# Where the weights of a feature-major product lie: 320 and 64 bytes from x modulo 512, in place of 448 for both parts

## The chip, the cores and the metric

The kernel runs on one core of a Trainium2 chip. The metric is the device time of one execution in microseconds, as the median of several runs. On-chip memory (SBUF) has 128 partitions; all addresses here are byte addresses within a partition. Engines: PE is TensorE (PEld its weight loads), DVE is VectorE, ACT is ScalarE, POOL is GpSimd, SP issues most DMAs.

## The reference

A decoder trunk of two pre-norm residual layers over 256 tokens and 2048 features, all in float32:

```
for l in range(2):
    h = rmsnorm(x, norm_mix[l])
    x = x + (even_mixer if l == 0 else odd_mixer)(h, ...)
    h = rmsnorm(x, norm_ffn[l])
    x = x + conv_ffn(h, ffn_w_up[l], ffn_conv_w[l], ffn_w_down[l])
return rmsnorm(x, norm_final)

def conv_ffn(h, w_up, conv_w, w_down):
    g, u = split(h @ w_up)              # 2048 -> 2 x 5632
    g = causal_dwconv(g, conv_w)        # width 3
    return (silu(g) * u) @ w_down       # 5632 -> 2048
```

The even mixer is a dilated-window attention of 8 heads beside a convolution module of 1024 channels; the odd mixer is an attention of 16 heads with forget gates. Each has an input projection and an output projection. Nearly all the work is products of a [256 x K] activation with a [K x N] weight matrix that is read once from memory, some 410 MB in all.

## The kernel before, in words

Each float32 product is made from two parts of each operand: hi is the operand rounded to the format that TensorE reads in one pass (float32r), lo is the rest. A product is hi·hi + hi·lo + lo·hi, three matmuls.

`stream` brings the weights. For each 1 MB piece of a panel of 512 columns it issues a DMA into a `raw` tile (three buffers), then twice takes a half of it: ACT copies it to `whi` (line 103), DVE subtracts to get `wlo` (line 104). Each of `whi` and `wlo` has four buffers of 4608 bytes per partition, 4096 of them used; `split_pair` cuts the used part out, from element `shift` on. Such a pair feeds 24 matmuls of a feature-major product, a piece 48.

There are two forms of product:

- Feature-major, `panel_b`: the weights (128 x 128) are the stationary operand and x (128 x 256 tokens) is streamed; the result has features on the partitions. For each of four column blocks and each k tile there is whi with the hi part of x (line 117), whi with the lo part of x (line 118), wlo with the hi part of x (line 119). A panel over all 16 k tiles is 192 matmuls. All projections but v, and the up products of both layers and the down product of layer 0, are made so. It takes its weights with `shift=SHIFT`, 16 elements.
- Token-major, `panel_a` and the last down product of layer 1: a 128 x 128 block of x is stationary and 512 columns of weights are streamed (lines 123 to 125). It takes its weights with shift 0. The last few matmuls, of acc_e, use weights in other rooms as well: the buffers of `gp`, `cv`, `hp` and `raw`, which the FFN has no more use for.

The x of a product is `xs` (the normed residual stream), `y` (the mixers' outputs) or `hp` (the FFN's hidden values), with hi and lo 1024 bytes apart. Small pads (`PADS`) put all three at the same place: each starts 64 bytes past a multiple of 512. So do the `whi` and `wlo` tiles, and since 4608 is nine times 512, all of their buffers. Steps inside them are multiples of 512 as well (a block of 128 float32 is 512 bytes). So the distance between x and weights modulo 512, x minus weights, is one number for all feature-major matmuls: 64 - (64 + 64) = 448 with a shift of 16 elements. For the token-major ones the streamed weights less the stationary x are 0, and in the rooms at the end also 480 and 448 (`whi` in `gp`, two buffers).

Order: the Tile scheduler sets the order of each engine's instructions when the program is built. TensorE runs the panels one after another; the next weights are copied and subtracted ahead of need. Between the matmuls of a panel stand a few small ones of norms and attention (for instance the four of `ss_f` and two of `bc_f` in the first panel of each FFN).

Of the kernel before, what the change touches and what calls it, by code (L numbers as in the profile page):

```python
# [29 lines left out]
KC = 2  # L30
NEG = -1.0e30
PADS = {"y0": 288, "mx1": 192, "ff0": 128, "ff1": 64}
SHIFT = 16
UP_GROUPS = ((0, 6), (6, 11))
TWO_PI_PARTS = (6.28125, 0.0019340515136718750, 1.2554228305816650e-06, 6.0796790328e-10)
MAGIC = 12582912.0
# [7 lines left out]
def trunk(ctx, tc, a):  # L44
# [14 lines left out]
    def misc(name):  # L59
        return pms.tile([P, 512], F32, tag="misc", name=name)  # L60
# [16 lines left out]
    def fill_in(after):  # L77
        pace[1] += pace[0]
        with tc.issue_after(after.ins), tc.high_priority(offset=-BEHIND):
            while waiting and pace[1] >= 1:  # L80
                waiting.pop(0)()
                pace[1] -= 1
        pace[1] = min(pace[1], 1.0)

    def split_pair(nm, half, width, shift):
        both = [wp.tile([P, KC * 512 + 128], F32R, tag=w, name=f"{w}_{nm}") for w in ("whi", "wlo")]
        return [t[:, shift:shift + KC * 512].rearrange("p (k c) -> p k c", k=half) for t in both]

    def stream(src_of, nk, width, name, dk=4, room=None, shift=0):

        half = KC * 512 // width
        for c in range(0, nk, dk * 512 // width):
            n = dk * 512 // width
            raw = wp.tile([P, 2 * KC * 512], F32, tag="raw", name=f"raw_{name}_{c}", bufs=3)
            rv = raw[:, :n * width].rearrange("p (k c) -> p k c", k=n)
            loads.append(nc.sync.dma_start(out=rv, in_=src_of(c, n)))
            for h in range(0, n, half):
                if room is None:
                    hi, lo = split_pair(f"{name}_{c + h}", half, width, shift)
                else:  # L100
                    hi, lo = room(f"{name}_{c + h}")
                with tc.high_priority(offset=AHEAD):
                    S.copy(hi, rv[:, h:h + half, :])  # L103
                    last = V.tensor_tensor(out=lo, in0=rv[:, h:h + half, :], in1=hi.bitcast(F32), op=ALU.subtract)  # L104
                fill_in(last)
                yield list(range(c + h, c + h + half)), hi, lo

    def panel_b(src_of, x2, kts, name, order=(0, 1, 2, 3), dk=4):

        acc = {m: pacc.tile([P, 512], F32, tag="acc", name=f"acc_{name}_{m}") for m in order}  # L110
        for ks, hi, lo in stream(src_of, len(kts), P * len(order), name, dk, shift=SHIFT):
            for m in order:
# [9 lines left out]
    def mm_a(o, hi, lo, xh, xl, first, last):  # L122
        PE.matmul(o, xh, hi, start=first, stop=False)  # L123
        PE.matmul(o, xh, lo, start=False, stop=False)  # L124
        PE.matmul(o, xl, hi, start=False, stop=last)  # L125

    def panel_a(src_of, x2, kts, name):

        acc = [pacc.tile([P, 512], F32, tag="acc", name=f"acc_{name}_{t}") for t in range(2)]
        for ks, hi, lo in stream(src_of, len(kts), 512, name):  # L130
            for t in range(2):
                ts = slice(t * P, (t + 1) * P)
                for j, k in enumerate(ks):
                    x = x2(kts[k])
                    mm_a(acc[t], hi[:, j, :], lo[:, j, :], x[:, 0, ts], x[:, 1, ts], k == 0, k == len(kts) - 1)
        return acc

    def cols(w, panel, k0=0):

        def part(c, n):  # L140
            kt = k0 // P + c
            return w[panel, kt // 4, :, kt % 4:kt % 4 + n, :]
        return part
# [123 lines left out]
    with ExitStack() as ph:  # L267
# [72 lines left out]
        with tc.high_priority(offset=400):  # L340
            for i in range(4):
                t, h = divmod(i, 2)
# [259 lines left out]
    def x_back():  # L602
        for kt in range(0, KT, 2):
            tx = misc(f"tb_{kt}")
            for t in range(2):
                for k in range(2):
                    PE.transpose(tx[:, t * T + k * P:t * T + (k + 1) * P], xT[:, kt + k, t * P:(t + 1) * P], ident)
            S.copy(o[:, :, kt * P:(kt + 2) * P], tx.rearrange("p (t c) -> p t c", t=2))
        S.dma_start(out=gb, in_=a["norm_final"].partition_broadcast(P))

    def add_o(acc, t, i):
        cs = slice(512 * i, 512 * (i + 1))
        V.tensor_tensor(out=o[:, t, cs], in0=acc, in1=o[:, t, cs], op=ALU.add)

    def down1(gi, w_dn, k0, kts, g2, fp):
        if gi == 0:
            x_back()
            for i in range(4):
                acc = panel_a(cols(w_dn, i, k0=k0), g2, kts, f"d1{gi}{i}")
                for t in range(2):  # L620
                    add_o(acc[t], t, i)
            return


        with tc.issue_after(copies[-1].ins):
            S.activation(dummy, ones[:, 0:1], AF.Sqrt)
        acc = [[None, None] for i in range(4)]
        for b, (i, t) in enumerate((i, t) for i in range(4) for t in range(2)):
            acc[i][t] = misc(f"acc_e{i}{t}") if b < 3 else pacc.tile([P, 512], F32, tag="acc", name=f"acc_e{i}{t}")
        n = len(kts)  # L630

        def rows(i, t, at, ks, hi, lo):
            for j, k in enumerate(ks):
                kt, ts = kts[at + k], slice(t * P, (t + 1) * P)
                mm_a(acc[i][t], hi[:, j, :], lo[:, j, :], g2(kt)[:, 0, ts], g2(kt)[:, 1, ts], at + k == 0, at + k == n - 1)

        def part(i, at, k, **kw):
            return stream(cols(w_dn, i, k0=k0 + at * P), k, 512, f"e{i}_{at}", dk=k, **kw)

        for at in range(0, n - 4, 4):  # L640
            for i in range(4):
                for got in part(i, at, 4):
                    for t in range(2):
                        rows(i, t, at, *got)


        def from_gate(nm):
            return [fp.tile([P, KC, 512], F32R, tag=tag, name=f"{w}_{nm}", bufs=2) for tag, w in (("gp", "whi"), ("cv", "wlo"))]

        def from_hidden(nm):  # L650
            both = fp.tile([P, 4, 2, T], F32R, tag="hp", name=f"wboth_{nm}", bufs=6).rearrange("p a b t -> p (a b t)")
            return [both[:, 1024 * h:1024 * (h + 1)].rearrange("p (k c) -> p k c", k=KC) for h in range(2)]

        def from_weights(nm):
            return split_pair(nm, KC, 512, 0)

        def from_raw(nm):
            both = wp.tile([P, 2 * KC * 512], F32, tag="raw", name=f"wboth_{nm}", bufs=3).bitcast(F32R)
            return [both[:, 1024 * h:1024 * (h + 1)].rearrange("p (k c) -> p k c", k=KC) for h in range(2)]

        rooms = [from_gate] * 2 + [from_hidden] + [from_weights] * 4 + [from_raw]
        at = n - 4
        last = [list(part(i, at, 4, room=lambda nm: rooms.pop(0)(nm))) for i in range(4)]
        for t in range(2):
            for i in range(4):
                for got in last[i]:
                    rows(i, t, at, *got)
                add_o(acc[i][t], t, i)
                cs = slice(512 * i, 512 * (i + 1))
                S.activation(junk[:, 512 * (i % 2):512 * (i % 2) + 512], o[:, t, cs], AF.Square, accum_out=fs[:, t, i:i + 1])  # L670
                if i < 3:
                    V.tensor_tensor(out=o[:, t, cs], in0=o[:, t, cs], in1=gb[:, cs], op=ALU.mult)
            V.reduce_sum(out=sf[:, t:t + 1], in_=fs[:, t, :], axis=AX.X)
            rf = rsqrt_cols(sf[:, t:t + 1], 1.0 / D, f"fin{t}", 1)
            for i in (1, 0, 3, 2):
                cs = slice(512 * i, 512 * (i + 1))
                if i == 3:
                    V.scalar_tensor_tensor(out=o[:, t, cs], in0=o[:, t, cs], scalar=rf, in1=gb[:, cs], op0=ALU.mult, op1=ALU.mult)
                elif i == 1:
                    V.tensor_scalar(out=o[:, t, cs], in0=o[:, t, cs], scalar1=rf, scalar2=None, op0=ALU.mult)  # L680
                else:
                    S.activation(o[:, t, cs], o[:, t, cs], AF.Copy, scale=rf)
                nc.sync.dma_start(out=a["out"][t * P:(t + 1) * P, cs], in_=o[:, t, cs])
# [63 lines left out]
```

## Time and profile before

| | |
|---|---|
| median of 3 runs | 2223.23 us (2222.28 to 2224.14) |
| the profiled execution | 2224.01 us, of which the trace spans 2222.2 |
| PE busy | 2202.4 us, 99%, 17,210 matmuls |
| PEld busy | 2132.0 us, 96% |
| DVE, ACT busy | 1407.7 us (63%), 1052.3 us (47%) |
| DMA | 414.61 MB, 187 GB/s in the mean |
| granted TensorE clock | 0.998 in the mean |

A matmul's duration in the profile is longer than the time from its start to the next one's, since matmuls are pipelined: a busy PE is not PE at its peak. The pace of a stretch is its length divided by the matmuls in it. A group's row gives the line, engine, operation, tiles and shapes, how often, then total and mean duration.

### The profile page before, as it was taken

The numbers are of one execution on the slowest core, as the hardware profiler recorded it, in microseconds if no ns is written. First come the engines' busy times: TensorE is split into PE (matmuls) and PEld (weight loads), VectorE is DVE, ScalarE is ACT, GpSimd is POOL, SyncE is SP. The second block draws the span as 40 slices with busy tenths as digits, with TensorE's granted clock in tenths as the row PEclk, the third lists the DMA queues.
The fourth block names the chain that finished last, engine by engine and source line by source line (L and its number), as shares of the span: only waits on it lengthen the run. The fifth ranks groups of instructions, "written<-read, shape, count | busy, mean of one in ns | idle before, by whom it ended". The sixth has DMA issues, their size and how long they took to land.

```text
span 2222.2 us, 40343 instructions
## 1 busy us (share of the span) xinstructions
PE 2202.4 (99%) x17210; PEld 2132.0 (96%) x17210; DVE 1407.7 (63%) x2105; ACT 1052.3 (47%) x1370; POOL 15.5 (1%) x50
## 2 busy tenths in 40 slices
PE   8999999999999999999999999999999999999998
PEld 8999999999999999999999999999999988999986
DVE  6999986666644566565655555566666544576645
ACT  7567675444433344444554444454444433444434
POOL 0000000000000000000000000000000000000000
PEclk9999999999999999999999999999999999999999
DMA  8554455555555555555544544555555555555553
GB/s 290 197 190 171 171 189 182 183 187 190 190 188 184 180 188 190 190 186 183 187 177 165 190 166 176 183 183 187 187 190 190 190 193 198 183 186 189 190 189 133
DMA packets 60260, 414.61 MB, mean 187 GB/s; under 512 B 7232, under 2 KB 7936, under 8 KB 11184
## 3 DMA queue, kind: packets, MB, share of 16 engines
q1 hardware_dynamic: 59328, 410.72, 51.6%
q8 instruction: 134, 2.20, 0.4%
q10 hardware_dynamic: 144, 1.05, 0.1%
q0 software_dynamic: 608, 0.26, 0.0%
q14 instruction: 46, 0.38, 0.0%
HBM read 409.84 MB, written 2.10 MB: 185 GB/s over the span
## 4 chain that ended last, share of the span: by engine, by line
PE 98%; DMA 1%; DVE 0%; ACT 0%; SPq 0%; issue 0%; ACTq 0%; DVEq 0%
PE acc_u L118 7%; PE acc_g L118 7%; PE acc_g L119 7%; PE acc_u L119 7%; PE acc_u L117 7%; PE acc_g L117 7%; PE acc_d L118 4%; PE acc_d L119 4%; PE acc_d L117 4%; PE acc_q L119 2%; PE acc_v L123 2%; PE acc_q L118 2%; PE acc_q L117 2%; PE acc_v L124 2%; PE acc_v L125 2%; PE acc_k L118 2%
## 5 line engine op out<-in xcount | busy, mean ns | idle before, releaser
L119 PE MATMUL acc_u<-xs,wlo_u 128*128 128x256 f32 x1408 | 394.7, 281 | 0.0
L118 PE MATMUL acc_u<-xs,whi_u 128*128 128x256 f32 x1408 | 394.7, 281 | 0.0
L117 PE MATMUL acc_g<-xs,whi_g 128*128 128x256 f32 x1408 | 394.5, 281 | 0.0
L118 PE MATMUL acc_g<-xs,whi_g 128*128 128x256 f32 x1408 | 394.5, 281 | 0.0
L119 PE MATMUL acc_g<-xs,wlo_g 128*128 128x256 f32 x1408 | 392.6, 281 | 0.0
L117 PE MATMUL acc_u<-xs,whi_u 128*128 128x256 f32 x1408 | 392.1, 281 | 0.0
L104 DVE TENSOR_TENSOR wlo_g<-raw_g,whi_g 128x1024 fp32r<-128x1024 f32 x176 | 215.4, 1224 | 186.2 <-ACT whi_g L103 186.2
L103 ACT CAST whi_u<-raw_u 128x1024 fp32r<-128x1024 f32 x176 | 184.8, 1050 | 279.6 <-PE acc_g L118 155.6
L103 ACT CAST whi_g<-raw_g 128x1024 fp32r<-128x1024 f32 x176 | 184.6, 1049 | 269.4 <-PE acc_u L118 114.4
L104 DVE TENSOR_TENSOR wlo_u<-raw_u,whi_u 128x1024 fp32r<-128x1024 f32 x176 | 214.8, 1220 | 109.5 <-ACT whi_u L103 109.5
L104 DVE TENSOR_TENSOR wlo_d<-raw_d,whi_d 128x1024 fp32r<-128x1024 f32 x136 | 166.5, 1224 | 176.2 <-ACT whi_d L103 176.2
L117 PEld LDWEIGHTS acc_g<-xs,whi_g 128*128 128x128 f32 x1408 | 268.5, 191 | 0.1
L117 PEld LDWEIGHTS acc_u<-xs,whi_u 128*128 128x128 f32 x1408 | 267.2, 191 | 0.0
L118 PEld LDWEIGHTS acc_g<-xs,whi_g 128*128 128x128 f32 x1408 | 265.9, 189 | 0.0
L118 PEld LDWEIGHTS acc_u<-xs,whi_u 128*128 128x128 f32 x1408 | 265.6, 189 | 0.0
L119 PEld LDWEIGHTS acc_u<-xs,wlo_u 128*128 128x128 f32 x1408 | 264.6, 188 | 0.0
L119 PEld LDWEIGHTS acc_g<-xs,wlo_g 128*128 128x128 f32 x1408 | 262.9, 188 | 0.1
L103 ACT CAST whi_d<-raw_d 128x1024 fp32r<-128x1024 f32 x136 | 142.9, 1051 | 219.7 <-PE acc_d L118 126.1
L117 PE MATMUL acc_d<-hp,whi_d 128*128 128x256 f32 x704 | 197.5, 281 | 0.0
L118 PE MATMUL acc_d<-hp,whi_d 128*128 128x256 f32 x704 | 197.5, 281 | 0.0
L119 PE MATMUL acc_d<-hp,wlo_d 128*128 128x256 f32 x704 | 196.5, 281 | 0.0
L117 PEld LDWEIGHTS acc_d<-hp,whi_d 128*128 128x128 f32 x704 | 135.1, 192 | 0.0
(311 smaller groups left out, 4946.7 us busy)
## 6 DMA issues: line engine op xcount, KB each, us to landing
raw_g<-in_ffn_w_up SPq DMA_DIRECT2D x88, 1024.0 KB, 4.8
raw_u<-in_ffn_w_up SPq DMA_DIRECT2D x88, 1024.0 KB, 4.8
raw_d<-in_ffn_w_down SPq DMA_DIRECT2D x68, 1024.0 KB, 4.8
raw_e<-in_ffn_w_down SPq DMA_DIRECT2D x20, 1024.0 KB, 4.8
raw_q<-in_od_w_in SPq DMA_DIRECT2D x16, 1024.0 KB, 4.8
raw_k<-in_od_w_in SPq DMA_DIRECT2D x16, 1024.0 KB, 4.8
raw_v<-in_od_w_in SPq DMA_DIRECT2D x16, 1024.0 KB, 4.8
raw_oc<-in_od_w_out SPq DMA_DIRECT2D x16, 1024.0 KB, 4.8
```

The costliest lines, as they stand in the source:

```text
L103: S.copy(hi, rv[:, h:h + half, :])
L104: last = V.tensor_tensor(out=lo, in0=rv[:, h:h + half, :], in1=hi.bitcast(F32), op=ALU.subtract)
L117: PE.matmul(o, hi[:, j, ms], x[:, 0, :], start=k == 0, stop=False)
L118: PE.matmul(o, hi[:, j, ms], x[:, 1, :], start=False, stop=False)
L119: PE.matmul(o, lo[:, j, ms], x[:, 0, :], start=False, stop=k == len(kts) - 1)
L123: PE.matmul(o, xh, hi, start=first, stop=False)
L124: PE.matmul(o, xh, lo, start=False, stop=False)
L125: PE.matmul(o, xl, hi, start=False, stop=last)
```

## The change

`SHIFT` becomes a pair, one number for whi and one for wlo, and `split_pair` takes one for each. 48 elements are 192 bytes: whi then starts at 64 + 192 = 256 modulo 512, and x minus whi is 64 - 256 = -192, that is 320 modulo 512. 112 elements are 448 bytes: wlo starts at 64 + 448 = 512, that is 0 modulo 512, and x minus wlo is 64. Where no shift is named (token-major products) both are 0, as before.

```diff
-SHIFT = 16
+
+SHIFT = (48, 112)
...
     def split_pair(nm, half, width, shift):
         both = [wp.tile([P, KC * 512 + 128], F32R, tag=w, name=f"{w}_{nm}") for w in ("whi", "wlo")]
-        return [t[:, shift:shift + KC * 512].rearrange("p (k c) -> p k c", k=half) for t in both]
+        return [t[:, s:s + KC * 512].rearrange("p (k c) -> p k c", k=half) for t, s in zip(both, shift)]
 
-    def stream(src_of, nk, width, name, dk=4, room=None, shift=0):
+    def stream(src_of, nk, width, name, dk=4, room=None, shift=(0, 0)):
...
-            return split_pair(nm, KC, 512, 0)
+            return split_pair(nm, KC, 512, (0, 0))
```

The built programs have the same instructions in the same order on each of the five engines, and the same tiles at the same addresses; only where in their buffers the weights of feature-major products start is another. Line numbers behind `SHIFT` are one higher in the changed kernel: what is line 117 before is line 118.

## The prediction

> **What bounds the kernel now.** I read the page first, for the busy shares and the chain; then the busy time by stretches, for the pace of the matmuls; then groups by line in short stretches, to see what makes the pace change; last the waits, for what a faster TensorE would run into.
>
> ```profile
> PE 2202.4 (99%) x17210; PEld 2132.0 (96%) x17210; DVE 1407.7 (63%) x2105; ACT 1052.3 (47%) x1370; POOL 15.5 (1%) x50
> PEclk9999999999999999999999999999999999999999
> PE 98%; DMA 1%; DVE 0%; ACT 0%; SPq 0%; issue 0%; ACTq 0%; DVEq 0%
> ```
>
> TensorE holds 98% of the chain at full clock in all 40 slices. No wait can be taken away; the time is the number of matmuls times the pitch from one start to the next. That pitch is not in the mean durations (matmuls overlap), but a long stretch in which PE never idles gives it: length over count.
>
> ```profile
> core 0: us, PE busy (x), PEclk, DMA share, GB/s
> 38.50:178.00 139.50, 139.50 (x1234) 1.00 0.56 198
> 294.70:344.70 50.00, 50.00 (x443) 1.00 0.53 190
> 350.60:1091.90 741.30, 741.30 (x6297) 1.00 0.52 187
> 1098.30:1134.50 36.20, 36.20 (x322) 1.00 0.53 190
> 1413.00:1456.00 43.00, 43.00 (x382) 1.00 0.54 192
> 1484.50:1743.00 258.50, 258.50 (x2197) 1.00 0.52 186
> 1757.90:1877.20 119.30, 119.30 (x528) 1.00 0.53 189
> 1878.00:2103.50 225.50, 225.50 (x1917) 1.00 0.53 187
> ```
>
> The count takes in the two or three matmuls that an edge cuts, so I take 2.5 off. First row: 139.50/1231.5 = 113.3 ns; third: 741.30/6294.5 = 117.8 ns; seventh, with 512 columns each (token-major products): 119.30/525.5 = 227.0 ns, that is 113.5 for 256 columns. So feature-major matmuls of one and the same form (128 weights, 256 columns) run at two paces, 113.3 and 117.8 ns, at the same clock and with the same traffic (187 to 198 GB/s). The slow pace is nearly all of the two FFN layers: rows three, six and eight. What switches it is seen in one panel, acc_g, ahead of and behind four tiny matmuls of the norm (ss_f, at 345.02 us). These are groups by line in 337.7 to 344.7 and then in 345.7 to 349.7:
>
> ```profile
> L117 PE MATMUL acc_g<-xs,whi_g 128*128 128x256 f32 x21 | 5.7, 276 | 0.0
> L118 PE MATMUL acc_g<-xs,whi_g 128*128 128x256 f32 x21 | 5.7, 276 | 0.0
> ...
> L117 PE MATMUL acc_g<-xs,whi_g 128*128 128x256 f32 x12 | 3.4, 281 | 0.0
> L118 PE MATMUL acc_g<-xs,whi_g 128*128 128x256 f32 x12 | 3.4, 281 | 0.0
> ```
>
> Same weights, same x, same addresses: 276 ns each before the interruption, 281 behind it, and then 281 for 740 us. So the pace is one that the stream of matmuls keeps once it has fallen into it; an interruption of a few matmuls can turn it over. The weight loads show it too. By line in 1413 to 1456 (fast) and in 700 to 743 (slow):
>
> ```profile
> L118 PEld LDWEIGHTS acc_oc<-y,whi_oc 128*128 128x128 f32 x127 | 23.8, 188 | 0.0
> L117 PEld LDWEIGHTS acc_oc<-y,whi_oc 128*128 128x128 f32 x127 | 23.8, 188 | 0.0
> ...
> L117 PEld LDWEIGHTS acc_d<-hp,whi_d 128*128 128x128 f32 x122 | 23.4, 192 | 0.0
> L119 PEld LDWEIGHTS acc_d<-hp,wlo_d 128*128 128x128 f32 x123 | 23.0, 188 | 0.0
> L118 PEld LDWEIGHTS acc_d<-hp,whi_d 128*128 128x128 f32 x122 | 22.9, 188 | 0.0
> ```
>
> At the slow pace one load of three lasts 192 ns instead of 188, and each matmul 5 ns longer. My reading, an inference and not something that these rows prove: the load of the next weights and the stream of x read SBUF side by side, and at the slow pace they keep meeting at places that can't serve both. That where they lie matters is shown nearest by the tail of the kernel, the only place where the distance between the streamed operand and the weights changes from matmul to matmul (0, 480, 448 modulo 512; everywhere else in the token-major products it is 0). The first row is a steady stretch, 2105 to 2190; the others are 2190.8 to 2193.4, and then two starts from the timeline:
>
> ```profile
> L124 PE MATMUL acc_e<-wlo_e,hp 128*128 128x512 f32 x126 | 49.0, 389 | 0.0
> ...
> L123 PE MATMUL acc_e<-whi_e,hp 128*128 128x512 f32 x4 | 1.6, 395 | 0.0
> L124 PE MATMUL acc_e<-wlo_e,hp 128*128 128x512 f32 x4 | 1.6, 395 | 0.0
> ...
> 2190.84 0.40 PE L123 MATMUL acc_e<-whi_e,hp 128*128 128x512 f32 x1
> 2193.40 0.39 PE L125 MATMUL acc_e<-whi_e,hp 128*128 128x512 f32 x1
> ```
>
> Eleven steps in 2.56 us are 232.7 ns, against 85.00 us over 374.5 matmuls, 227.0, in the steady stretch:
>
> ```profile
> 2105.00:2190.00 85.00, 85.00 (x377) 1.00 0.55 198
> ```
>
> **The change, part by part.** It adds, removes and moves no instruction on any engine. It gives 15,216 feature-major matmuls (64 panels of 192, and 768 + 2,112 + 48 in the output, down and gate products) other distances between weights and x: 320 for the two with whi (L117, L118 now), 64 for the one with wlo (L119), where all three had 448. The 1,632 token-major matmuls keep theirs.
>
> The term: what share of these runs at which pitch. Now slow, from the three long rows: 6,294.5 + 2,194.5 + 1,914.5 = 10,403 matmuls; and by their 281 ns durations some 600 more in short pieces like the one at 345.7. The difference of the pitches is 117.77 - 113.3 = 4.47 ns. If all go fast: 11,000 x 4.47 = 49.2 us less. If all go slow: the other 15,216 - 11,000 = 4,200 pay 4.47: 18.8 us more. If the tail's price is paid on each, 232.7 - 227.0 = 5.7 ns above the fast pitch: 86.7 - 49.2 = 37.5 us more. These are the ends; a gain of more than 49 has no row, since 113.3 is also half of the token-major pitch, where the weight load fills only half of the time.
>
> I take the fast end. The slow pace needs an arrangement that meets again in each matmul; with all three distances equal, a step that meets once repeats in each of the next thousands, which is what the 741 us show. With two distances half of 512 apart, the load of wlo and those of whi don't come to x at the same point, and a meeting in one isn't handed on to the next. The tail speaks against this (changing distances cost there), but its distances change with every new buffer, while here they repeat every three matmuls, as a lock needs.
>
> Copies and subtractions, at other start addresses:
>
> ```profile
> L104 DVE TENSOR_TENSOR wlo_g<-raw_g,whi_g 128x1024 fp32r<-128x1024 f32 x176 | 215.4, 1224 | 186.2 <-ACT whi_g L103 186.2
> L103 ACT CAST whi_u<-raw_u 128x1024 fp32r<-128x1024 f32 x176 | 184.8, 1050 | 279.6 <-PE acc_g L118 155.6
> raw_g<-in_ffn_w_up SPq DMA_DIRECT2D x88, 1024.0 KB, 4.8
> ```
>
> Nothing for these: ACT waits for PE to free a whi buffer (155.6 us in one group alone), so they are done ahead of need. Were they 5% longer, some 60 ns, they would still fit: one pair serves 24 matmuls, 2.7 us, against 1.22 us of DVE and 1.05 of ACT. **What is late next** at the fast pitch: a 1 MB load serves 48 matmuls, 5.44 us instead of 5.65, and lands in 4.8; the first row of stretches ran so at 198 GB/s. In the FFN, DVE has more to do than there:
>
> ```profile
> core 0: us, PE busy (x) PEld busy (x) DVE busy (x) ACT busy (x) POOL busy (x), PEclk, DMA share, GB/s
> 345.00:609.00 264.00, 264.00 (x2242) 263.95 (x2241) 168.27 (x245) 113.28 (x124) 0.63 (x6) 1.00 0.52 186
> ```
>
> 64% busy becomes 66%. So nothing gives the 49 us back.
>
> **The sum.** The profiled execution took 2224.0 us (span 2222.2 and 1.8 around it). 2224.0 - 49.2 = 2174.8; the median of the runs, 2223.2, lies 0.8 lower: 2174.0. I add 1 us for short slow pieces behind interruptions, which cost 4.47 ns for each of some 200 matmuls: 2175.
>
> **Rivals.**
> *No change.* The stall doesn't depend on the distance; the pace is turned by the interruptions alone, at the same places: 2223. For it: the switch at 345 happens without any change of address. Against it: the tail. The Trainium skill, "SBUF — State Buffer", section "Who interferes with whom", says that TensorE reads its moving operand and its weights through two independent ports and that PE never waits on anyone; by that rule the change is worth nothing. The trace bears it out for DMA and the other engines (both paces at the same traffic), but not inside PE, where 276 became 281 at one clock.
>
> *A part of it.* The slow pace stays possible and each entry is thrown anew. The first long stretch is worth 6,294.5 x 4.47 = 28.1 us, the second 9.8, the third 8.6. If only the first goes fast: 2195; if only the two others do: 2205. For it: in the trace the same product leaves interruptions both ways (fast from 1098.3, slow from 350.6).
>
> *Slower: it never locks.* Since the distance changes twice in three matmuls, the streams are pushed each time, in the mixers too, which are fast now. By the slow pitch for all: 2223.2 + 18.8 = 2242; by the tail's price: 2223.2 + 37.5 = 2261. It decides from 49.2 us/15,216 = 3.2 ns in each matmul on. For it: the tail, which pays 5.7 for as long as its distances change. Against it: a third of the matmuls there have distance 0 beside 480 or 448, no regular cycle, and it lasts a few matmuls only.
>
> **How the numbers follow.** All fast 0.45 (its own range 2171 to 2184: the pitch difference read 0.1 ns wrong is 1 us, some pieces stay slow); a part 0.15 (2190 to 2215); no change 0.13; slower 0.27 (2235 to 2265). A measurement here can tell about 0.2%, 4.4 us, from no change. Faster 0.60, same 0.13, slower 0.27. The range 2171 to 2252 leaves out the upper half of the slower case and a little below.
>
> **What would show it.** Right: the FFN stretches at 113.3 ns (a window of 741 us there would hold some 6,540 matmuls), acc_g, acc_u and acc_d at 276 ns, all weight loads at 188, token-major groups as before at 389. A part: some FFN panels at 276, others at 281, with the turn at an interruption. Wrong: acc_ag, acc_q, acc_k and acc_oc above 276 (never locks), or the FFN still at 281. Should the FFN be fast and the time not fall by 49, DVE or the loads of raw have become late, and matmuls would show idle time ahead of them.

## The result, and the profile after

The changed kernel takes 2239.63 us (median of 3, 2239.49 to 2240.41) against 2223.23: the ratio is 1.0067, with a 95% interval of 1.0053 to 1.0082. The forecast was 2175; what came is the rival "slower", by the first of its two prices (2242). The page first, then the busy time by stretches (columns as before):

```profile
PE 2218.6 (99%) x17210; PEld 2148.0 (96%) x17210; DVE 1409.2 (63%) x2105; ACT 1052.0 (47%) x1370; POOL 15.6 (1%) x50
PE 98%; DMA 0%; DVE 0%; ACT 0%; SPq 0%; issue 0%; ACTq 0%; DVEq 0%
```

```profile
38.50:178.00 139.50, 139.50 (x1187) 1.00 0.56 196
360.00:1090.00 730.00, 730.00 (x6201) 1.00 0.53 187
1426.00:1470.00 44.00, 44.00 (x376) 1.00 0.53 186
1500.00:1758.00 258.00, 258.00 (x2193) 1.00 0.53 185
1773.00:1892.00 119.00, 119.00 (x527) 1.00 0.54 190
1894.00:2118.00 224.00, 224.00 (x1904) 1.00 0.53 185
```

With 2.5 taken off each count, the first row is 117.8 ns per matmul where it was 113.3; the third, acc_oc, 117.8, which was 113.3 as well. The FFN rows stay at 117.8, the token-major row at 226.9. So no feature-major stretch is fast any more. The interruption by ss_f and the weight loads show that this isn't quite the slow pace of before; groups by line ahead of the interruption (343.9 to 351.5), behind it (352.3 to 356.5), then weight loads in 700 to 743:

```profile
L118 PE MATMUL acc_g<-xs,whi_g 128*128 128x256 f32 x22 | 6.1, 280 | 0.0
...
L118 PE MATMUL acc_g<-xs,whi_g 128*128 128x256 f32 x13 | 3.6, 280 | 0.0
...
L119 PEld LDWEIGHTS acc_d<-hp,whi_d 128*128 128x128 f32 x122 | 22.9, 188 | 0.0
L120 PEld LDWEIGHTS acc_d<-hp,wlo_d 128*128 128x128 f32 x122 | 22.8, 188 | 0.0
L118 PEld LDWEIGHTS acc_d<-hp,whi_d 128*128 128x128 f32 x122 | 22.8, 187 | 0.0
```

The interruption turns nothing over now, a matmul lasts 280 ns on both sides (281 and 276 before), and no group of loads is at 192. The pitch is the same 117.8 ns.

### The profile page after: what moved, and what is told of

The parts are those of the page before. It is cut to its first block, busy times and chain, and to the rows that moved or that the text cites. A ratio compares the mean times of both kernels' runs of the same rounds, so it can differ in the third digit from the quotient of the medians.

```text
span 2237.7 us, 40343 instructions
## 1 busy us (share of the span) xinstructions
PE 2218.6 (99%) x17210; PEld 2148.0 (96%) x17210; DVE 1409.2 (63%) x2105; ACT 1052.0 (47%) x1370; POOL 15.6 (1%) x50
## 4 chain that ended last, share of the span: by engine, by line
PE 98%; DMA 0%; DVE 0%; ACT 0%; SPq 0%; issue 0%; ACTq 0%; DVEq 0%
PE acc_g L120 8%; PE acc_u L120 7%; PE acc_u L119 7%; PE acc_g L119 7%; PE acc_g L118 7%; PE acc_u L118 7%; PE acc_d L120 4%; PE acc_d L119 4%; PE acc_d L118 4%; PE acc_q L120 2%; PE acc_q L118 2%; PE acc_k L118 2%; PE acc_k L120 2%; PE acc_k L119 2%; PE acc_q L119 2%; PE acc_v L124 2%
## 5 line engine op out<-in xcount | busy, mean ns | idle before, releaser
L118 PE MATMUL acc_g<-xs,whi_g 128*128 128x256 f32 x1408 | 392.1, 279 | 0.0
L118 PE MATMUL acc_u<-xs,whi_u 128*128 128x256 f32 x1408 | 389.3, 279 | 0.0
L104 ACT CAST whi_u<-raw_u 128x1024 fp32r<-128x1024 f32 x176 | 184.8, 1050 | 279.5 <-PE acc_g L119 155.7
L119 PEld LDWEIGHTS acc_u<-xs,whi_u 128*128 128x128 f32 x1408 | 264.7, 188 | 0.0
L119 PEld LDWEIGHTS acc_g<-xs,whi_g 128*128 128x128 f32 x1408 | 264.6, 188 | 0.0
L118 PEld LDWEIGHTS acc_g<-xs,whi_g 128*128 128x128 f32 x1408 | 263.4, 187 | 0.1
L118 PEld LDWEIGHTS acc_u<-xs,whi_u 128*128 128x128 f32 x1408 | 261.9, 187 | 0.0
L118 PE MATMUL acc_d<-hp,whi_d 128*128 128x256 f32 x704 | 196.1, 279 | 0.0
```

The costliest lines, as they stand in the source:

```text
L118: PE.matmul(o, hi[:, j, ms], x[:, 0, :], start=k == 0, stop=False)
L119: PE.matmul(o, hi[:, j, ms], x[:, 1, :], start=False, stop=False)
```

## The experiments

In each table and sentence below a place is a distance x minus weights, and pitches are from the row 400 to 1000 of the stretches (FFN of layer 0), the count less 2.5. Every kernel differs from the changed one by the lines shown alone.

**Both parts at one place, and one part changed at a time.**

```diff
-SHIFT = (48, 112)
+SHIFT = (48, 48)     # both at 320
+SHIFT = (112, 112)   # both at 64
+SHIFT = (48, 16)     # whi at 320, wlo at 448
+SHIFT = (16, 112)    # whi at 448, wlo at 64
```

> SHIFT = (48, 48): both parts at 320. Theory 'equal distances' (the pace of 113.3 ns needs whi and wlo at one distance, whichever): fast pieces come back, acc_k or acc_oc at 113.3 ns, 2175 to 2230 us. Theory 'the value 448' (the pace of 113.3 ns exists at the distance 448 alone): all feature-major matmuls at 117.8 ns, 2240 us. Theory 'whi decides' (two of three loads): 320 is the place that spoils it, 2240 us. Theory 'wlo decides': 64 was the place that spoils it, fast pieces come back.

> SHIFT = (112, 112): both parts at 64. 'Equal distances': fast pieces at 113.3 ns, 2175 to 2230 us. 'The value 448': 117.8 ns throughout, 2240 us. 'Whi decides': 64 for whi not tried so far, either. 'Wlo decides': 117.8 ns throughout, 2240 us.

> SHIFT = (48, 16): whi moved to 320, wlo left at 448. 'Equal distances' and 'the value 448': 117.8 ns throughout, 2240 us. 'Whi decides': 2240 us. 'Wlo decides': the fast pieces of the kernel before, in the mixers, 2223 us.

> SHIFT = (16, 112): whi left at 448, wlo moved to 64. 'Equal distances' and 'the value 448': 117.8 ns throughout, 2240 us. 'Whi decides': the fast pieces of the kernel before, 2223 us. 'Wlo decides': 2240 us.

Measured: 2241.02 us (ratio 1.0066, 1.0051 to 1.0081), 2241.23 (1.0067, 1.0052 to 1.0082), 2176.39 (0.9777, 0.9761 to 0.9794) and 2174.80 (0.9772, 0.9757 to 0.9786). One row of stretches of each, in this order:

```profile
400.00:1000.00 600.00, 600.00 (x5096) 1.00 0.52 187
```

```profile
400.00:1000.00 600.00, 600.00 (x5097) 1.00 0.52 187
```

```profile
38.50:178.00 139.50, 139.50 (x1232) 1.00 0.55 199
400.00:1000.00 600.00, 600.00 (x5296) 1.00 0.54 194
```

```profile
400.00:1000.00 600.00, 600.00 (x5296) 1.00 0.54 194
```

That is 117.8 ns twice and 113.35 twice. All four theories fell: none had the two unequal pairs at 2175, and either half of the change made alone gives what the prediction had expected of the whole. One thing orders all the kernels so far: 320 and 64 are the same place modulo 256, namely 64, and 448 is 192. Then the change, both at 320 and both at 64 are one and the same arrangement (64 with 64), the fast two are 64 with 192, and the kernel before is 192 with 192.

**Is the period 256, and what is needed for the fast pace?**

```diff
-SHIFT = (48, 112)
+SHIFT = (16, 80)   # 448 and 192: both 192 modulo 256
+SHIFT = (0, 32)    # 0 and 384: 0 and 128
+SHIFT = (16, 32)   # 448 and 384: 192 and 128
+SHIFT = (0, 0)     # both 0
```

> SHIFT = (16, 80): whi at 448, wlo at 192, that is 256 bytes apart. After the first four kernels three theories are left. 'Period 256, apart by 128' (only distances modulo 256 count; whi and wlo 128 apart are fast, whi and wlo at one place are not): both parts are at 192 modulo 256, as in the kernel before, so the same mixture of 113.3 and 117.8 ns and the same 2223 us. 'One part at 448, the other elsewhere' (what the two fast kernels share): 113.3 ns throughout, 2175 us. 'Any pair of places but 320 with 64': 2175 us.

> SHIFT = (0, 32): whi at 0, wlo at 384, that is 128 apart, neither at 448. 'Period 256, apart by 128': 113.3 ns throughout, 2175 us. 'One part at 448': 117.8 ns throughout, 2240 us. 'Any pair but 320 with 64': 2175 us.

> SHIFT = (16, 32): whi at 448, wlo at 384, 64 apart. 'Period 256, apart by 128' says nothing certain of 64: fast if any distance apart will do, 2175 us; between 2175 and 2240 if it takes 128. 'One part at 448' and 'any pair but 320 with 64': 2175 us.

> SHIFT = (0, 0): both parts at 0, the distance of the token-major products. 'Period 256, apart by 128': not fast throughout, 2200 to 2241 us, a mixture or all slow. 'One part at 448, the other elsewhere': 2240 us. If instead 0 is a good place by itself, as the token-major pitch of 226.7 ns would suggest: 2175 us.

Measured: 2224.14 us (0.9987, 0.9976 to 0.9997), 2261.01 (1.0153, 1.0138 to 1.0168), 2248.17 (1.0094, 1.0079 to 1.0109) and 2273.98 (1.0211, 1.0196 to 1.0226).

```profile
38.50:178.00 139.50, 139.50 (x1227) 1.00 0.56 200
400.00:1000.00 600.00, 600.00 (x5097) 1.00 0.52 187
```

```profile
400.00:1000.00 600.00, 600.00 (x5040) 1.00 0.52 184
```

```profile
400.00:1000.00 600.00, 600.00 (x5078) 1.00 0.52 187
```

```profile
400.00:1000.00 600.00, 600.00 (x5003) 1.00 0.51 183
```

and of this last kernel, the weight loads between 700 and 743:

```profile
L120 PEld LDWEIGHTS acc_d<-hp,wlo_d 128*128 128x128 f32 x121 | 23.1, 192 | 0.0
L119 PEld LDWEIGHTS acc_d<-hp,whi_d 128*128 128x128 f32 x120 | 23.0, 192 | 0.0
L118 PEld LDWEIGHTS acc_d<-hp,whi_d 128*128 128x128 f32 x119 | 22.9, 192 | 0.0
```

The first of the four, with parts 256 bytes apart, has the pieces of the kernel before: 113.9 ns in the mixer, with the end of the start-up in it (the granted clock was 0.74 from 38.5 to 41; from 50 on the row has 113.3), and 117.8 in the FFN. Its ten executions lie at two levels, 2223 to 2225 and 2230, as do those of the kernel before beside it (2224 to 2225 and 2228 to 2231), in other shares. So a period of 256 fits all kernels so far; 128 doesn't, since 64 and 192 would then be one place. But "apart by 128" fell at the next kernel: 119.1 ns; 64 apart gives 118.2, both at 0 gives 120.0, where all three groups of weight loads last 192 ns. A pitch that is good for token-major products (distance 0, 227 ns) says nothing for these.

**x moved instead of the weights, one more tiny matmul in the interruption, and the last equal place.**

```diff
 # whi at 320, wlo at 448, hp moved by 64 bytes
-PADS = {"y0": 288, "mx1": 192, "ff0": 128, "ff1": 64}
-SHIFT = (48, 112)
+PADS = {"y0": 288, "mx1": 192, "ff0": 192, "ff1": 128}
+SHIFT = (48, 16)
 # the kernel before, bc_f twice
+SHIFT = (16, 16)
         PE.matmul(bc[:, :T], ones, dg, start=True, stop=True)
+        if name[0] == "f":
+            PE.matmul(bc[:, :T], ones, dg, start=True, stop=True)
 # the kernel before, ss_f twice
+SHIFT = (16, 16)
-        for t in range(2):
+        for t in (0, 1, 0, 1) if name[0] == "f" else (0, 1):
 # both at 384
+SHIFT = (32, 32)
```

> SHIFT = (48, 16), the kernel that ran at 113.3 ns throughout (2176 us), with the pad ahead of the FFN's tiles 64 bytes longer: the weights and xs stay where they are, hp alone moves by 64 bytes. Distances of acc_d become 384 and 0; all others stay 320 and 448. Theory 'distance to x': the 2,112 acc_d matmuls of layer 0 leave 113.3 ns for 118 to 121 ns (whi and wlo at 128 and 0 modulo 256 was slow with the parts exchanged), 10 to 16 us more, 2185 to 2192 us; acc_g and acc_u stay at 113.3. Rival 'place of the weights alone', or of weights to raw: acc_d stays at 113.3 ns, 2176 us.

> SHIFT = (16, 16), the kernel before, with the small matmul bc_f of each FFN done twice into the same place (one more float32 matmul of 256 columns in the interruption of each first panel, nothing else). Theory 'the interruption throws the pace anew': one or both FFN stretches behind it turn to 113.3 ns: 2195 us (first and its down product), 2214 (second), or as before if the throw falls the same way. Rival 'the pace belongs to the product': 2223 us, acc_g, acc_u and acc_d at 281 ns.

> SHIFT = (16, 16), the kernel before, with the four small ss_f matmuls of each FFN done twice (eight instead of four). 'The interruption throws the pace anew': the 39 matmuls behind it at 276 ns or again at 281, and by that another arrival at bc_f: 2195 to 2224 us. 'The pace belongs to the product': 2223 us.

> SHIFT = (32, 32): both parts at 384, the last of the four places modulo 256 for equal parts (0 gave 120.0 ns, 64 gave 117.8, 192 both paces). No theory gives its pitch; from the neighbours 64 and 192, 113.3 to 117.8 ns, and from 0 and 128 together with 0 or 192, 118 to 120: 2240 to 2274 us.

*hp moved:* 2195.35 us (0.9860, 0.9846 to 0.9875), 19 more than with hp in its place. Stretches in the up products (acc_g, acc_u), in acc_d of layer 0, and in the token-major acc_d of layer 1:

```profile
400.00:590.00 190.00, 190.00 (x1679) 1.00 0.55 195
620.00:710.00 90.00, 90.00 (x762) 1.00 0.52 186
1740.00:1840.00 100.00, 100.00 (x430) 1.00 0.52 188
```

113.3 ns, 118.5 ns and 233.9 ns. No weight of acc_d moved, and it left the fast pace by 5.2 ns; 2,112 x 5.2 = 11 us, as expected. The rest of the 19, which takes the time out of the expected 2185 to 2192, I had not counted: by the same pad the token-major products with hp went from a distance of 0 to 448, and from 227 to 234 ns; some 1,050 x 7 = 7 us. So the place of the weights alone doesn't decide, for a streamed x or for a stationary one.

Is it the distance, or the place of hp by itself? In the tail the same pad moves some weights together with x, those in the rooms `gp`, `cv` and `hp`. Four starts of the kernel before, then the same four matmuls here. The first two bound 12 steps with weights in such rooms, the last two 18 steps with weights in whi and wlo, which stayed:

```profile
2192.23 0.39 PE L123 MATMUL acc_e<-whi_e,hp 128*128 128x512 f32 x1
2195.01 0.39 PE L123 MATMUL acc_e<-whi_e,hp 128*128 128x512 f32 x1
2196.39 0.39 PE L123 MATMUL acc_e<-whi_e,hp 128*128 128x512 f32 x1
2200.47 0.39 PE L123 MATMUL acc_e<-wboth_e,hp 128*128 128x512 f32 x1
...
2162.88 0.39 PE L124 MATMUL acc_e<-whi_e,hp 128*128 128x512 f32 x1
2165.67 0.39 PE L124 MATMUL acc_e<-whi_e,hp 128*128 128x512 f32 x1
2167.06 0.39 PE L124 MATMUL acc_e<-whi_e,hp 128*128 128x512 f32 x1
2171.26 0.39 PE L124 MATMUL acc_e<-wboth_e,hp 128*128 128x512 f32 x1
```

Where both moved, the 12 steps last 2.78 and 2.79 us; where x alone moved, the 18 go from 4.08 to 4.20 us, from 226.7 to 233.3 ns each. That speaks for the distance. For feature-major matmuls no run moves both.

*bc_f twice:* 2189.12 us (0.9841, 0.9820 to 0.9861), 36 us less, with every distance as in the kernel before and one more bc_f in each FFN (two matmuls in the trace: 17,214 in all against 17,210). Groups ahead of the interruption (345.7 to 349.7) and behind it (351.7 to 356), then stretches:

```profile
L118 PE MATMUL acc_g<-xs,whi_g 128*128 128x256 f32 x12 | 3.4, 281 | 0.0
...
L118 PE MATMUL acc_g<-xs,whi_g 128*128 128x256 f32 x13 | 3.6, 276 | 0.0
```

```profile
360.00:1050.00 690.00, 690.00 (x6091) 690.00 (x6090) 428.04 (x579) 303.36 (x334) 0.97 (x9) 1.00 0.55 194
1490.00:1700.00 210.00, 210.00 (x1855) 210.00 (x1855) 139.61 (x202) 92.51 (x102) 0.54 (x5) 1.00 0.55 194
1842.50:2060.00 217.50, 217.50 (x1849) 217.50 (x1848) 138.20 (x196) 91.37 (x99) 0.32 (x3) 1.00 0.52 186
```

Both stretches behind a bc_f run at 113.3 ns now; the third, which no bc_f precedes, stays at 117.8. 28.1 + 9.8 = 37.9 was the prediction's price for these two. That the pace belongs to the product is ruled out: with both parts at 192 an interruption throws it.

*ss_f twice:* 2227.71 us (1.0009, 0.9980 to 1.0037), no difference; the matmuls between ss_f and bc_f stayed at 281 ns (L118 in 351.5 to 355.5) and the FFN stayed slow. The profiled execution took 2230.5, and its row for the first mixer is slow, though nothing was edited there:

```profile
39.00:179.00 140.00, 140.00 (x1191) 1.00 0.54 193
```

117.8 ns. The throw isn't the same in each execution, then: the thirteen of the kernel before beside this one lie between 2205.2 and 2230.7 us. *Both at 384:* 2256.45 us (1.0138, 1.0121 to 1.0155), 118.7 ns:

```profile
400.00:1000.00 600.00, 600.00 (x5059) 1.00 0.52 185
```

**The place 448, or the pair 192 and 64?** Both fast kernels had one part at 448.

```diff
-SHIFT = (48, 112)
+SHIFT = (80, 48)   # whi at 192, wlo at 320
```

> SHIFT = (80, 48): whi at 192, wlo at 320, neither at 448. 'Period 256' with the map measured so far (192 and 64 modulo 256 is the pair that ran at 113.3 ns throughout): 113.3 ns throughout, 2175 us. Rival 'one part has to lie at 448 and the other at 320 or 64', which the two fast kernels leave open: 117.8 ns or slower, 2240 us or more.

2176.44 us (0.9777, 0.9761 to 0.9794), fast in mixers and FFN alike:

```profile
38.50:178.00 139.50, 139.50 (x1233) 1.00 0.56 200
400.00:1000.00 600.00, 600.00 (x5296) 1.00 0.54 194
```

The map modulo 256, of the whi and wlo distances in the FFN of layer 0:

| whi, wlo | ns per matmul | us |
|---|---|---|
| 64, 192 and 192, 64 (three kernels) | 113.35 | 2174.8 to 2176.4 |
| 192, 192 (before; 448 with 192) | 117.8 | 2223.2, 2224.1 |
| 192, 192, bc_f twice | 113.3 | 2189.1 |
| 64, 64 (the change; both 320; both 64) | 117.8 | 2239.6 to 2241.2 |
| 192, 128 | 118.2 | 2248.2 |
| 128, 0 (acc_d alone, hp moved) | 118.5 | 2195.4 |
| 128, 128 | 118.7 | 2256.5 |
| 0, 128 | 119.1 | 2261.0 |
| 0, 0 | 120.0 | 2274.0 |

Other pairs weren't tried. The best versions are thus the three with 64 and 192; a change of one of the two numbers, `SHIFT = (16, 112)` at 2174.8 us or `(48, 16)`, is enough, and their intervals overlap. They aren't quite alike: with whi at 64 and wlo at 192, `(48, 16)`, a matmul (L118) in the short piece between ss_f and bc_f, 345.9 to 349.5, lasts 279 ns; with the parts exchanged, 277 and 276 in the two kernels.

## Why the prediction was wrong

*The pace that an interruption can turn over, its size and place:* right. Giving all the slow stretches the fast pitch was put at 49.2 us; the three kernels that do it gain 49 to 51 us against the runs of the kernel before beside them. The price of the single stretches fits too (37.9 against 36 with bc_f twice). "Same weights, same x, same addresses" is true of the two pieces around ss_f only modulo 512: they are other k tiles, in other buffers. DVE, ACT and the loads kept up with the faster TensorE, as reckoned. That the weight load fills only half of the time in token-major products has no row (loads are busy 98.75 of the 119.30 us from 1757.9), but no run got under 113.3 ns either.

*The step that failed* is "I take the fast end", with its reason: "with two distances half of 512 apart, the load of wlo and those of whi don't come to x at the same point". It took the modulus of 512, in which the two distances of the change are stated, for the period of the pace, without a row for it. The runs fit a period of 256: 320 and 64 are one place, and the change didn't separate the two parts at all. It moved both from 192 to 64, a place where the fast pace wasn't seen in any stretch, behind any interruption. The reason was doubly weak: unequal distances alone don't bring the fast pace either (192 with 128, 0 with 128). The tail was weaker evidence than it was read for, too: its six steps with weights in hp, at distance 0, last 1.39 us (2193.62 to 2195.01), 232 ns each like the ones at 480 and 448, so the distance modulo 512 doesn't explain its price. And "all weight loads at 188" was no sign of the fast pace: the changed kernel has them at 187 and 188 and is slow.

*The rival that came true* had the right price and a wrong ground. "By the slow pitch for all", 18.8 us, is what happened: the traces differ by 2237.7 - 2222.2 = 15.5 us, the runs by 16.4. But it isn't that the distance changes twice in three matmuls. Where it really does, with 64 and 192, the matmuls are at their fastest. The tail's price (5.7 ns on each) didn't apply here. That the new place has the very pitch of the old slow pace, 117.8 ns, was luck: other places measured 118.2 to 120.0. That 18.8 was 3 us too much lies in the count. By the starts of the same matmuls in both traces, the changed kernel gains 0.7 us in the start-up (up to 34 us), loses 16.2 in the mixers, and loses nothing in the FFN. That is 4.47 ns for some 3,600 matmuls, not for 4,200: those of the start-up, for one, weren't at 113.3 (194 at 138 ns each).

*No change:* by the Trainium skill's rule ("SBUF — State Buffer", section "Who interferes with whom") that the ports for weights and moving operand are independent and PE waits on nobody, no distance should cost time. The measurement says otherwise: the distance alone moved the time from 2175 to 2274 us, with the same instructions. Whether the two ports get in each other's way is not shown. *A part of it* is how the kernel before behaves by itself from one execution to another. One of its executions took 2205.2 us, which is the price of that rival for the second and third stretch; no trace of it was kept.

What stays open is the mechanism. That weight loads and the streamed operand meet in SBUF would explain why the distance counts and why the loads last 192 ns at 0 with 0. But at 64 with 64 the pace is slow and no group of loads is longer, no run shows the meeting itself, and none shows why 64 with 192 is fast.

## What to carry to other kernels

Where TensorE is the chain and its matmuls follow without a gap, compare the pitch of equal matmuls over stretches before anything else; two pitches at one clock are time to be had, here 2.2% for one start address. Before reasoning on addresses, find the period by one pair of kernels that must be equal under it, and change the parts one at a time: the two halves of this change were worth 49 and 51 us, and together they cost 16. A gain that hangs on how an interruption falls, as with 192 and 192, isn't one to keep; a pair that was fast in every long stretch, and within 2.4 us in its four executions, is.

## What the runs showed of the hardware that was not expected

- The pitch of float32r matmuls with 128 weights and 256 columns goes from 113.35 to 120.0 ns with where the weights start, as distances of x from whi and wlo modulo 256 bytes; with 512 streamed columns, from 227 to 234 ns (distance 0 and 448).
- At one distance, 192 for both parts, two pitches are stable for hundreds of microseconds, and one more bc_f (two small matmuls) between them turned one into the other: 36 us of 2225.
- The same kernel, unchanged, can be thrown otherwise from one execution to the next: 2205.2 to 2230.7 us.
